# One input load of a dilated convolution split into sixteen DMAs, fourteen of them of two or three partitions

## The chip, the cores and the metric

The kernel runs on one NeuronCore of a Trainium2 chip. The metric is device time in microseconds, the median of several runs; less is better. Beside it stands a profile of one execution, whose span runs from the first to the last instruction.

## The reference

A 3x3 convolution with dilation 2 and padding 2, in float32: x is 16 x 64 x 64 x 64 (batch, channels in, rows, columns), weight 128 x 64 x 3 x 3, the output 16 x 128 x 64 x 64.

```python
for b in range(batch):
    for co in range(c_out):
        for ci in range(c_in):
            for kh in range(k):
                for kw in range(k):
                    output[b, co] += weight[co, ci, kh, kw] * x_pad[b, ci, kh*dilation:kh*dilation+h, kw*dilation:kw*dilation+w]
```

## The kernel before

Two images make a pair: their 2 x 64 input channels fill the 128 partitions, so there are `NP` = 8 pairs (0 to 7). A pair's input is a tile `x16` of 128 partitions x 64 rows x 64 columns in float16. Pair 0 comes as float32 in two DMAs from SyncE (L75) into a tile `x32` and is converted on VectorE and ScalarE; the others come by one DMA each from GpSimd's queue, which converts from float32 on the way (`load`, L78 to L81). A whole load reads 16 KB and writes 8 KB per partition.

The three kernel rows are computed with a trick that saves matmuls: GpSimd adds rows that lie two apart in the image (`prepare`, L141, tile `s16`), two instructions for a pair, for image rows 0 to 36 and 36 to 64. PE multiplies these sums with the middle kernel row (phase "w1"), and the rows themselves with differences of kernel rows (the other two phases). ScalarE copies the first phase from PSUM to SBUF (L204), and VectorE adds that copy to each of the two other phases and writes the output tile `o` (L209). A pair is walked in `NU` = 4 steps `u` of three phases each. All matmuls are issued on L186. The output tile of a pair is 4 MB and leaves by SyncE's queue: whole for pairs 0 to 4 (L221), by image for pairs 5 and 6, and by image and half for pair 7 (L224).

The buffers set how far engines may run ahead: `x16pool` has 6 tiles, `sumpool` (the sums) 3, `opool` (the outputs) 3. Pairs 1 to 4 are loaded near the start. Pairs 5, 6 and 7 are loaded two pairs ahead, at step u = 1 of pairs 3, 4 and 5 (L195), just in front of the two `prepare` calls of the next pair on GpSimd's queue. The order of the instructions on each engine is that of the program. Since GpSimd has to wait for PE only when a sum buffer is to be used again, it runs well ahead of PE: it fills the sums of pair p + 3 as soon as those of pair p have been read. Each DMA that GpSimd issues reports its landing on one of eight semaphores, taken in turn; a DMA that takes a semaphore again waits for the DMA that had it before.

Of the kernel before, what the change touches and what calls it, by code (L numbers as in the profile page):

```python
# [10 lines left out]
def kernel(  # L11
# [7 lines left out]
    nc = tc.nc  # L19

    B, CI, H, W = x.shape
# [5 lines left out]
    P = 128  # L27
    f32 = mybir.dt.float32
    f16 = mybir.dt.float16
    NP = B // 2  # L30
# [19 lines left out]
    x16pool = ctx.enter_context(tc.tile_pool(name="x16pool", bufs=6))  # L50
# [9 lines left out]
    x_pair = x.rearrange("(nb two) c h w -> nb (two c) h w", two=2)  # L60
# [5 lines left out]
    x16 = {}  # L66
# [11 lines left out]
    def load(pb, cuts):  # L78
        x16[pb] = x16pool.tile([P, H, W], f16, tag="x16", name=f"x16_{pb}")
        for lo, hi in zip(cuts, cuts[1:]):  # L80
            nc.gpsimd.dma_start(out=x16[pb][:, lo:hi], in_=x_pair[pb, :, lo:hi])  # L81

    AHEAD = 5

# [15 lines left out]
    for name, a in (("w21", 2), ("w01", 0)):  # L100
        for u in range(2):
            eng = nc.vector if name == "w21" else nc.gpsimd
            eng.tensor_sub(  # L103
                out=w16[:, SLOT[name] * KW : (SLOT[name] + 1) * KW, u, :],
                in0=w32k[:, a * KW : (a + 1) * KW, :],
                in1=w32k[:, KW : 2 * KW, :],
            )

            if name == "w01" and u == 0:
                load(1, [0, H])  # L110

    w_sb = wpool.tile([P, NS * KW, CO], f16, name="w_sb")
    for n, name in enumerate(("w1", "w21", "w0", "w01", "w2")):
        ps = cpool.tile([P, 2, NB], f32, tag="ps", name=f"wt{n}")
        k0 = SLOT[name] * KW
        for j in range(KW):
            nc.tensor.matmul(  # L117
                out=ps[:, 0, j * CO : (j + 1) * CO],
# [16 lines left out]
    def prepare(pb, lo, hi):  # L135
        if pb not in s16:
            s16[pb] = sumpool.tile([P, 2 * NQ, W], f16, tag="s16", name=f"s16_{pb}")
        src = (x16[pb] if pb else x32).rearrange("p (q e r) w -> p q e (r w)", e=2, r=2)
        dst = s16[pb].rearrange("p (q r) w -> p q (r w)", r=2)
        q0, q1 = lo // 4, hi // 4  # L140
        nc.gpsimd.tensor_add(  # L141
            out=dst[:, q0:q1], in0=src[:, q0:q1, 0, :], in1=src[:, q0:q1, 1, :]
        )

    prepare(0, 0, 20)
    for pb in range(2, AHEAD):
        load(pb, [0, H])
# [33 lines left out]
    def phase(pb, u, terms):  # L181

        ps = cpool.tile([CO, 2, NB], f32, tag="ps", name="ps")
        for pair in zip(*(conv(pb, hb, ps[:, hb], u, terms) for hb in range(2))):
            for m in pair:
                nc.tensor.matmul(**m)  # L186
        return ps

    BOTH = NP - 3
    for pb in range(NP):  # L190
        o = opool.tile([P, 2, H, W], f32, tag="o", name=f"o{pb}")
        ov = o.rearrange("p b (q e r) w -> p b q e (r w)", e=2, r=2)
        for u in range(NU):

            if u == 1 and AHEAD <= pb + 2 < NP:  # L195
                load(pb + 2, [0, H])
            if pb + 1 < NP:
                if u == 1:
                    prepare(pb + 1, 0, 36)
                elif u == 2:  # L200
                    prepare(pb + 1, 36, H)

            s32 = spool.tile([P, 2, NB], f32, tag="s32", name="s32")
            nc.scalar.copy(out=s32, in_=phase(pb, u, [("w1", 2, 0)]))  # L204
            for e, terms in enumerate(
                ([("w21", 1, 0), ("w0", 1, -1)], [("w01", 0, 0), ("w2", 0, 1)])
            ):
                ps = phase(pb, u, terms)
                nc.vector.tensor_add(  # L209
                    out=ov[:, :, u * UQ : (u + 1) * UQ, e, :],  # L210
                    in0=ps.rearrange("p b (q c) -> p b q c", c=QW),
                    in1=s32.rearrange("p b (q c) -> p b q c", c=QW),
                )

            step = NU // 2 if pb == NP - 1 else NU
            if (u + 1) % step == 0:
                fl = slice((u + 1 - step) * 4 * UQ, (u + 1) * 4 * UQ)
                if pb < BOTH:  # L220
                    nc.sync.dma_start(out=out_pair[pb], in_=o)  # L221
                else:
                    for hb in range(2):
                        nc.sync.dma_start(out=out[2 * pb + hb, :, fl], in_=o[:, hb, fl])  # L224
# [35 lines left out]
```

## Time and profile before

| | before |
|---|---|
| time, median of 3 runs | 126.64 us (126.33 to 126.74) |
| span of the profiled execution | 124.3 us |
| PE busy | 105.2 us (85%) |
| VectorE busy | 80.8 us (65%) |
| ScalarE busy | 39.6 us (32%) |
| GpSimd busy | 41.4 us (33%) |
| DMA moved | 43.42 MB in 3961 packets |
| HBM read, written | 17.07 MB, 33.55 MB |
| a load by GpSimd's queue, issue to landing | 16.0 us (median of 7) |

The span is that of one execution, from its first to its last instruction; the timed runs cover some time around it as well, and no time of the profiled execution apart from its span was recorded. "Busy" leaves out the issuing of DMAs. DMA bytes are counted as written: a load that converts float32 to float16 counts half of what it reads. "q0 software_dynamic" is the queue of the DMAs that GpSimd issues, "q1 hardware_dynamic" that of SyncE. Of the queues the profile gives packets, bytes and the time that the packets took as a share of the 16 DMA engines' time; in a window these are the packets that start in it. A line of the windows' table has for each engine the busy time in that stretch and the number of instructions, then the clock that PE was granted, the mean busy share of the 16 DMA engines, and the rate. A line of the timeline has start and duration, the engine, the line of the kernel, the operation, and in brackets the idle time before it and what ended it.

### The profile page before, as it was taken

The numbers are of one execution on the slowest core, as the hardware profiler recorded it, in microseconds if no ns is written. First come the engines' busy times: TensorE is split into PE (matmuls) and PEld (weight loads), VectorE is DVE, ScalarE is ACT, GpSimd is POOL, SyncE is SP. The second block draws the span as 40 slices with busy tenths as digits, with TensorE's granted clock in tenths as the row PEclk, the third lists the DMA queues.
The fourth block names the chain that finished last, engine by engine and source line by source line (L and its number), as shares of the span: only waits on it lengthen the run. The fifth ranks groups of instructions, "written<-read, shape, count | busy, mean of one in ns | idle before, by whom it ended". The sixth has DMA issues, their size and how long they took to land.

```text
span 124.3 us, 2244 instructions
## 1 busy us (share of the span) xinstructions
PE 105.2 (85%) x981; PEld 55.7 (45%) x981; DVE 80.8 (65%) x71; ACT 39.6 (32%) x40; POOL 41.4 (33%) x33
## 2 busy tenths in 40 slices
PE   6357999999999999999999999999999999960000
PEld 2043555555555555555555555555555555520000
DVE  0470199787778777877769778777877787770000
ACT  4760823333333333333333333333332433320000
POOL 2859998794095009500930093000000000000000
PEclk9999999999999999999999999999999999999655
DMA  4999999999999999999999999999999999999991
GB/s 129 346 359 218 214 214 216 224 237 411 393 327 314 332 306 319 316 390 314 324 345 427 425 427 432 422 427 427 432 438 427 432 414 432 427 417 419 422 406 71
DMA packets 3961, 43.42 MB, mean 349 GB/s; under 512 B 368, under 2 KB 368, under 8 KB 624
## 3 DMA queue, kind: packets, MB, share of 16 engines
q1 hardware_dynamic: 2944, 35.95, 68.9%
q0 software_dynamic: 1008, 7.34, 28.4%
q8 instruction: 7, 0.11, 0.3%
q14 instruction: 2, 0.02, 0.0%
HBM read 17.07 MB, written 33.55 MB: 407 GB/s over the span
## 4 chain that ended last, share of the span: by engine, by line
PE 80%; DMA 5%; POOL 2%; DVE 1%; DVEq 1%; SPq 0%; issue 0%
PE ps L186 80%; DMA x<-in_x_dram 5%; POOL s L141 2%; DVE o L209 1%; DVEq L255 1%; SPq L64 0%; DVEq L209 0%
## 5 line engine op out<-in xcount | busy, mean ns | idle before, releaser
L209 DVE TENSOR_TENSOR o<-ps,s 128x1024 f32<-128x1024 f32 x64 | 76.7, 1223 | 25.9 <-PE ps L186 16.8
L186 PE MATMUL ps<-x,w_sb 64*128 64x496 f16 (+3 forms) x768 | 85.3, 368 | 0.0
L186 PEld LDWEIGHTS <-w_sb 64*128 64x128 f16 x960 | 53.4, 95 | 49.3 <-issue 3.7
L204 ACT COPY s<-ps 128x1024 f32<-128x1024 f32 x32 | 32.4, 1012 | 63.0 <-PE ps L186 63.0
L141 POOL TENSOR_TENSOR s<-x 128x1152 f16<-128x1152 f16 (+4 forms) x18 | 35.1, 1971 | 31.1 <-PE ps L186 28.3
L186 PE MATMUL ps<-s,w_sb 64*128 64x496 f16 (+1 forms) x192 | 26.5, 379 | 2.1 <-POOL s L141 2.1
L81 POOL DMA_DIRECT2D x<-in_x_dram x7 | 4.0, 579 | 0.0
L132 ACT CAST x<-x 128x1024 f16<-128x1024 f32 (+1 forms) x3 | 2.8, 973 | 3.4 <-DMA x<-in_x_dram 3.4
L93 PE MATMUL warm<-zero 128*128 128x512 f16 x6 | 2.7, 630 | 1.2 <-DVE zero L87 1.2
L117 PE MATMUL wt<-ident,w 128*128 128x128 f16 x15 | 1.8, 312 | 2.1 <-ACT w L99 2.1
L103 DVE TENSOR_TENSOR w<-w 128x192 f16<-128x192 f32 x2 | 1.5, 800 | 2.5 <-DMA w<-in_weight_dram 2.5
L117 PEld LDWEIGHTS <-w 128*128 128x128 f16 x15 | 1.5, 146 | 3.0 <-ACT w L99 3.0
L99 ACT CAST w<-w 128x576 f16<-128x576 f32 x2 | 2.3, 1222 | 1.6 <-DMA w<-in_weight_dram 1.6
L103 POOL TENSOR_TENSOR w<-w 128x192 f16<-128x192 f32 x2 | 1.9, 951 | 2.4 <-DMA w<-in_weight_dram 2.4
L126 DVE CAST w_sb<-wt 128x384 f16<-128x384 f32 x3 | 1.6, 552 | 1.4 <-PE wt L117 1.4
L93 PEld LDWEIGHTS <-zero 128*128 128x128 f16 x6 | 0.7, 138 | 2.3 <-DVE zero L87 1.2
L99 ACT ACT_TABLE_LOAD x1 | 1.3, 1283 | 0.7 <-PEq L241 0.7
L128 ACT CAST w_sb<-wt 128x384 f16<-128x384 f32 x2 | 1.0, 478 | 1.1 <-PE wt L117 1.1
L130 DVE CAST x<-x 128x1280 f16<-128x1280 f32 x1 | 0.8, 826 | 0.5 <-DMA x<-in_x_dram 0.5
L87 DVE MEMSET zero<- 128x256 uint32 x1 | 0.3, 272 | 0.9 <-PEq L241 0.9
masks.py:199 POOL TENSOR_SCALAR_AFFINE_SELECT ident<-ident 128x128 f16<-128x128 f16 x1 | 0.3, 292 | 0.1
masks.py:197 POOL MEMSET ident<- 128x128 f16 x1 | 0.2, 204 | 0.3 <-POOLq L241 0.3
(4 smaller groups left out, 0.4 us busy)
## 6 DMA issues: line engine op xcount, KB each, us to landing
out_dram<-o SPq DMA_DIRECT2D x5, 4096.0 KB, 21.6
out_dram<-o SPq DMA_DIRECT2D x4, 2048.0 KB, 12.4
x<-in_x_dram POOLq DMA_DIRECT2D x7, 1024.0 KB, 16.0
out_dram<-o SPq DMA_DIRECT2D x4, 1024.0 KB, 10.6
x<-in_x_dram SPq DMA_DIRECT2D x1, 1152.0 KB, 6.5
x<-in_x_dram SPq DMA_DIRECT2D x1, 896.0 KB, 10.6
w<-in_weight_dram SPq DMA_DIRECT2D x1, 288.0 KB, 2.9
```

The source lines that it names most:

```text
L81: nc.gpsimd.dma_start(out=x16[pb][:, lo:hi], in_=x_pair[pb, :, lo:hi])
L93: nc.tensor.matmul(out=warm[:, 0], lhsT=zero[:, 0:P], rhs=zero, start=True, stop=True)
L99: nc.scalar.copy(out=w16[:, 0:NK, u, :], in_=w32k)
L103: eng.tensor_sub(out=w16[:, SLOT[name] * KW : (SLOT[name] + 1) * KW, u, :], in0=w32k[:, a * KW : (a + 1) * KW, :], in1=w32k[:, KW : 2 * KW ...
L117: nc.tensor.matmul(out=ps[:, 0, j * CO : (j + 1) * CO], lhsT=w16[:, k0 + j, :, :].rearrange("o t i -> o (t i)"), rhs=ident, start=True, st ...
L126: nc.vector.tensor_copy(out=dst, in_=ps[:, 0, 0 : KW * CO])
L132: nc.scalar.copy(out=x16[0][:, lo:hi], in_=x32[:, lo:hi])
L141: nc.gpsimd.tensor_add(out=dst[:, q0:q1], in0=src[:, q0:q1, 0, :], in1=src[:, q0:q1, 1, :])
L186: nc.tensor.matmul(**m)
L204: nc.scalar.copy(out=s32, in_=phase(pb, u, [("w1", 2, 0)]))
L209: nc.vector.tensor_add(out=ov[:, :, u * UQ : (u + 1) * UQ, e, :], in0=ps.rearrange("p b (q c) -> p b q c", c=QW), in1=s32.rearrange("p b ( ...
L255: with _tile.TileContext(nc) as tc:
```

## The change

The load of the last pair (7) goes through a new function. Instead of one DMA for the whole tile it issues sixteen: rows 0 to 60 of all 128 partitions; rows 60 to 64 of the first 112 partitions; and these four rows of the last 16 partitions twice half by half: the left 32 columns by eight DMAs of two partitions, the right 32 columns by five DMAs of three partitions and one of the single partition left. All pieces together cover the tile once. Nothing else is touched.

```diff
+    def load_tagged(pb):
+        x16[pb] = x16pool.tile([P, H, W], f16, tag="x16", name=f"x16_{pb}")
+        lo, p1 = H - 4, P - 16
+        parts = [(0, P, 0, lo, 0, W), (0, p1, lo, H, 0, W)]
+        for n, c in ((2, 0), (3, W // 2)):
+            parts += [
+                (p, min(n, P - p), lo, H, c, c + W // 2) for p in range(p1, P, n)
+            ]
+        for p, n, r, r1, c, c1 in parts:
+            nc.gpsimd.dma_start(
+                out=x16[pb][p : p + n, r:r1, c:c1],
+                in_=x_pair[pb, p : p + n, r:r1, c:c1],
+            )
...
             if u == 1 and AHEAD <= pb + 2 < NP:
-                load(pb + 2, [0, H])
+                if pb + 2 < NP - 1:
+                    load(pb + 2, [0, H])
+                else:
+                    load_tagged(pb + 2)
```

## The prediction

> **What bounds the kernel now.** I read the 40 slices first, then a table of windows, the DMA queues in three windows, the chain, and GpSimd's instructions in order of time.
>
> ```profile
> PE   6357999999999999999999999999999999960000
> DMA  4999999999999999999999999999999999999991
> GB/s 129 346 359 218 214 214 216 224 237 411 393 327 314 332 306 319 316 390 314 324 345 427 425 427 432 422 427 427 432 438 427 432 414 432 427 417 419 422 406 71
> ```
>
> PE stops in slice 36 of 40; the DMA engines are full from the second slice to the last but one. The GB/s dip in the first half only because loads are counted by what they write: they read float32 and write half as many bytes (8 loads read the 16.8 MB that are nearly all of "HBM read 17.07 MB"). Slices 4 to 8 at 214 to 218 written are about 430 read, the same as the outputs' 427.
>
> ```profile
> core 0: us, PE busy (x) PEld busy (x) DVE busy (x) ACT busy (x) POOL busy (x), PEclk, DMA share, GB/s
> 64.00:80.00 16.00, 16.00 (x157) 8.47 (x155) 13.19 (x12) 5.06 (x5) 4.21 (x2) 1.00 1.01 425
> 112.00:120.00 8.00, 0.00 (x0) 0.00 (x0) 0.01 (x1) 0.00 (x0) 0.00 (x0) 0.72 1.01 425
> 120.00:124.30 4.30, 0.00 (x0) 0.00 (x0) 0.00 (x0) 0.00 (x0) 0.00 (x0) 0.50 0.34 143
> ```
>
> After 112 us only DMA runs: 8.0 x 425 + 4.3 x 143 is 4.0 MB. The last two outputs (2.1 MB) are issued at 112.04, so 1.9 MB is queued ahead of them, 4.5 us at 427 GB/s. The chain says PE 80%, but it starts from the last engine instruction: PE, VectorE and all in front of them may slip 4.5 us before the DMA engines run dry. So the time is total work of the DMA engines over their rate, on the engine that ends last. The last window is uneven: mean busy there is 0.34 x 4.3 = 1.5 us, yet something runs to nearly 124, so an average engine ends some 2 us before the last.
>
> **Time.** The page gives only the span, 124.3 us; the timed runs have a median of 126.64, so 2.3 us lie around it. I add to both alike. One measurement of this kernel can tell about 0.3%, 0.38 us, from no change.
>
> **The change.** Pair 7's load, one DMA, becomes 16: 60 rows of 128 partitions, four rows of 112, then 8 DMAs of two partitions and 6 of at most three, each 4 rows x 32 columns. The bytes are the same. Three things are added.
>
> *GpSimd's time and waits.* Its part of the trace:
>
> ```profile
> 46.58 4.21 POOL L141 TENSOR_TENSOR s<-x 128x1152 f16<-128x1152 f16 x2 [7.65 <-PE ps L186]
> 50.73 0.57 POOL L81 DMA_DIRECT2D x<-in_x_dram  x1
> 58.95 4.21 POOL L141 TENSOR_TENSOR s<-x 128x1152 f16<-128x1152 f16 x2 [7.65 <-PE ps L186]
> 71.31 4.21 POOL L141 TENSOR_TENSOR s<-x 128x1152 f16<-128x1152 f16 x2 [8.14 <-PE ps L186]
> ```
>
> The load is issued at 50.73, right after pair 5's sums; GpSimd then sits idle until PE frees a sum buffer at 58.95. Fifteen more issues at 0.57 are 8.6 us (535 to 697 ns in the group's rows). But the order of the changed kernel shows more: GpSimd's DMAs share eight semaphores in turn, so the ninth to sixteenth DMA of this load each wait for an earlier DMA on their semaphore. The eighth waits for load 6 (issued 38.36, 17.5 us to landing, 55.9); the ninth for the 60-row DMA, which landed as a whole load after 16.0 us, at 66.7. Behind it on GpSimd are pair 6's sums and then pair 7's. Eight issues from 66.7 end at 71.3. If each of the six small DMAs queued by then lands one by one behind output packets, two turns of 0.61 us each, it is 66.7 + 7.3 + 0.6 = 74.6. Pair 6's sums then end at 75.5 to 78.8 instead of 63.2. PE runs from 9.95 for 99.61 us, 12.45 a pair, and wants them at 84.7; pair 7's sums (at most 4.2 us plus some 6 us until the last small DMA has landed, about 85 to 89) are wanted at 97.1. Cover: 6 us on the first, 8 on the second, and 4.5 us more of queued output behind both. Cost zero; without cover it would be a microsecond per microsecond.
>
> *Waits on PE.* Two weight loads and a matmul of pair 7 wait for eight semaphores where none stood; VectorE's queue shows 21 ns for such a wait, so 0.2 us, below the 4.5 us of queued output. Zero.
>
> *DMA work.* This has no cover: the engines are full. The packet counts:
>
> ```profile
> DMA packets 392, 2.83 MB, mean 217 GB/s; under 512 B 48, under 2 KB 48, under 8 KB 48
> q0 software_dynamic: 391, 2.81, 103.6%
> ...
> DMA packets 703, 10.73 MB, mean 429 GB/s; under 512 B 48, under 2 KB 48, under 8 KB 48
> q1 hardware_dynamic: 701, 10.70, 100.3%
> ...
> DMA packets 143, 0.37 MB, mean 284 GB/s; under 512 B 13, under 2 KB 13, under 8 KB 133
> q1 hardware_dynamic: 143, 0.37, 97.5%
> ```
>
> These are the queues in 12 to 25 us (loads alone), 75 to 100 (outputs alone) and 1.6 to 2.9 (the weights' rows of 2.3 KB). The page's 368 packets under 512 B are 16 for each of its 23 DMAs: one completion per engine.
>
> - Completions: 15 DMAs more, 15 on each engine if small ones also post 16. Price: the loads carry 48 of them to 343 data packets, the outputs 48 to 653, yet they read 432 GB/s (2 x 2.81 MB in 13 us) against 429. So the floor is zero; half a per cent of a 0.61 us packet over the difference of 0.07 a packet gives 0.045 us at most. I take 0.02, the middle: 0.30 us (0 to 0.7).
> - Small packets: 16 partitions x 4 rows x 2 halves, 128 of 128 B read, 8 on each engine if evenly spread. By bytes alone 128 B cost 0.005 us (0.613 us for 16 KB in the second window); the weights' packets cost 0.975 x 1.3 x 16 / 143 = 0.142. I take 0.04, nearer to the completions, whose size is nearer: 0.32 us (0.04 to 1.1).
> - The 112-partition piece: 7 packets more an engine at 0.01, its bytes being the same: 0.07 (0 to 0.3).
>
> The sum is 0.69 us, with ends of 0.04 and 2.1: 126.64 + 0.7 = 127.3, span 125.0.
>
> The Trainium skill (DMA: Bandwidth & Descriptors, section Anatomy of one DMA — SWDGE (gpsimd) path) gives a DMA of this kind a fixed cost of about 2.0 us; if that held the engines, 15 more DMAs would make 30 us and the kernel about 157. The trace speaks against it as a cost of engine time: in 12 to 25 us one load follows another at 432 GB/s read. It can only lengthen landings.
>
> **Rivals.**
>
> *Nothing measurable (0.17):* the completions are free and small packets cost little beyond bytes; 0.04 to 0.3 us, 126.8. For it: no window shows a price of a completion. Against: no row shows 128 B packets at the price of their bytes, and the weights' rows run at 284 GB/s.
>
> *Not slower (0.12): the last engine is relieved.* The end belongs to the engine that finishes last, and an average one has 2 us left. Should that engine have carried the last 16 partitions, and the small DMAs now go to others, it loses up to its whole share of the four rows: 8 partitions x 1 KB of read, half a packet, 0.31 us; 126.3. This decides from the point where its 15 completions cost under 0.02 each. The uneven last window speaks for it; nothing shows which engine is last.
>
> *Small pieces pile up on few engines (0.13).* If a two-partition DMA always goes to the first two engines and a three-partition one to the first three, the first engine gets 14 x 4 = 56 small packets: 56 x 0.04 + 0.37 = 2.6 us. On the last engine that is 129.2; on an average one, 2 us of it vanish in its slack: 127.2. Middle 128.2. No row of this profile has a DMA under 128 partitions, so it can't be excluded.
>
> The Trainium skill (same page, section Why a DMA increments its semaphore by 16 and not by 1) has both: few engines from a cursor that moves on, or, for some direct copies, one partition to an engine from the first on; by the first the pieces come out even, 127.3, by the second it is this rival. It also says that all 16 engines post a completion whatever the shape, as I assumed; no row here shows it for small ones.
>
> *GpSimd comes too late (0.05).* If each of the eight waits took far longer than two turns, pair 6's first sums would start after 82.2 and PE would stall; only beyond 4.5 us of stall, GpSimd free at 86.7, does it reach the end. At 89 it would be 2.3 us: 126.64 + 0.7 + 2.3 = 129.6. Against: 12 us to spare.
>
> That the pieces would not be there is no rival: the order of instructions has all 16.
>
> **How the numbers follow.** Even spread with priced packets has 0.53 and gives the time, 127.3, its own range 126.7 to 128.7. Slower: 0.51 of it, all of piling up (0.13) and of late GpSimd (0.05), 0.03 of the third case: 0.72. Same: 0.02 + 0.14 + 0.03 of relief = 0.19. Faster: 0.09 of relief, its 0.31 us being close to 0.38 and the runs lying 0.4 us apart. The range 126.5 to 128.8 leaves out most of relief, the upper half of piling up and late GpSimd: 0.2.
>
> **What would show it.** Packets up from 3961 to about 4441, those under 512 B from 368 to 736 (16 x 38 + 128); DMA slices still full, PE's end within a microsecond of 109.6, and the drain after it longer by the sum. GpSimd: eight issues from 50.7, a gap until about 66, eight more, pair 6's sums at 71 to 75. Wrong would be: a PE wait for the sums, a DMA slice below full, a drain of unchanged length (packets free), or completions that don't grow by 16 a DMA.

## The result, and the profile after

The changed kernel takes 131.25 us (median of 4 runs) against 126.48 before (four runs now as well): 4.77 us more by the medians. Medians here and below are over all runs, while a ratio leaves out a kernel's runs that lie over 1.5% above its fastest, here the one of 132.64: it is 1.0346 with a 95% interval of 1.031 to 1.0382, which is 4.4 us. The forecast was 127.3 and its range ended at 128.8. The profiled execution has a span of 129.7 us, 5.4 more than the 124.3 of before.

The slices of the page, the changed kernel:

```profile
PE   6289999999999999999999999930899999993000
...
PEclk9999999999999999999999999995589999999855
DMA  4999999999999999999999999999999607999993
GB/s 129 366 329 210 217 212 215 220 280 419 336 328 321 308 323 331 349 337 295 368 411 430 425 415 430 425 420 420 430 435 410 253 8 323 455 435 387 422 412 157
```

Three things are new, in this order of time: a hole in PE's row, a fall of the clock granted to PE right behind it, and a hole in the DMA row, with 8 GB/s in one slice. The same stretches as a table of windows (stretch, its length, busy time of PE, PE's weight loads, VectorE, ScalarE and GpSimd with their instructions, PE's clock, DMA share, GB/s):

```profile
84.00:88.00 4.00, 1.48 (x16) 0.76 (x13) 2.35 (x2) 0.20 (x1) 0.54 (x1) 1.00 1.03 430
88.00:92.00 4.00, 0.63 (x4) 0.30 (x5) 0.00 (x0) 0.00 (x0) 3.59 (x3) 0.50 0.99 418
92.00:96.00 4.00, 4.00 (x28) 1.90 (x26) 0.95 (x1) 1.01 (x1) 3.46 (x2) 0.65 1.02 426
96.00:104.00 8.00, 8.00 (x80) 4.11 (x76) 6.33 (x6) 2.43 (x3) 0.00 (x0) 1.00 0.84 343
104.00:108.00 4.00, 4.00 (x44) 2.16 (x40) 2.93 (x3) 1.62 (x2) 1.89 (x1) 1.00 0.15 63
```

PE does 2.1 us of work in the eight from 84 to 92, and the DMA engines go dry from 102 to 108, when the outputs of that time should have left. Why PE stands still, GpSimd's instructions in order of time say, here from the eighth of the sixteen issues on (the first seven start at 49.96):

```profile
55.23 0.54 POOL L92 DMA_DIRECT2D x<-in_x_dram  x1 [1.41 <-DMA x<-in_x_dram]
65.99 0.54 POOL L92 DMA_DIRECT2D x<-in_x_dram  x1 [10.22 <-DMA x<-in_x_dram]
71.24 0.54 POOL L92 DMA_DIRECT2D x<-in_x_dram  x1 [4.71 <-DMA x<-in_x_dram]
74.27 0.55 POOL L92 DMA_DIRECT2D x<-in_x_dram  x1 [2.49 <-DMA x<-in_x_dram]
76.74 0.55 POOL L92 DMA_DIRECT2D x<-in_x_dram  x1 [1.92 <-DMA x<-in_x_dram]
79.80 0.54 POOL L92 DMA_DIRECT2D x<-in_x_dram  x1 [2.52 <-DMA x<-in_x_dram]
82.87 0.54 POOL L92 DMA_DIRECT2D x<-in_x_dram  x1 [2.53 <-DMA x<-in_x_dram]
85.33 0.54 POOL L92 DMA_DIRECT2D x<-in_x_dram  x1 [1.93 <-DMA x<-in_x_dram]
88.39 0.54 POOL L92 DMA_DIRECT2D x<-in_x_dram  x1 [2.52 <-DMA x<-in_x_dram]
88.95 6.50 POOL L155 TENSOR_TENSOR s<-x 128x1152 f16<-128x1152 f16 x3
```

The last nine issues wait for landings, 30.2 us in all, and pair 6's sums start at 88.95 instead of 58.95. The list of waits and the chain complete it:

```profile
PE ps L200 <- POOL s L155: 5.9, 1, 5.9
...
88.95 2.38 POOL s L155
...
91.37 25.49 PE ps L200 x228
```

The packets that made the landings late are in the table of queues, first over the span, then from 75 to 88 us:

```profile
DMA packets 5162, 43.43 MB, mean 335 GB/s; under 512 B 1456, under 2 KB 1568, under 8 KB 1952
q0 software_dynamic: 2208, 7.34, 28.1%
...
q1 hardware_dynamic: 354, 5.54, 100.0%
q0 software_dynamic: 354, 0.00, 1.8%
```

GpSimd's queue has 1200 packets more than the 1008 of before, where the forecast had 480. From 75 to 88 us it and the outputs' queue start 354 packets each. This reads as turns: a packet of 4 to 64 bytes, then an output packet of 16 KB, and so on.

The theory formed on this, called A in the experiments: every small packet takes one turn behind an output packet of 0.61 us; a small DMA has five of them on every engine; GpSimd, whose DMAs wait for landings on their eight semaphores, is therefore late with pair 6's sums; PE stalls, and the outputs' queue runs dry. Rival B: the added packets' own work on the DMA engines makes the time, as in the forecast, at a higher price.

### The profile page after: what moved, and what is told of

It is laid out like the page before. It is cut to its first block, busy times and chain, and to the rows that moved or that the text cites. A ratio compares the mean times of both kernels' runs of the same rounds, so it can differ in the third digit from the quotient of the medians.

```text
span 129.7 us, 2266 instructions
## 1 busy us (share of the span) xinstructions
PE 107.7 (83%) x981; PEld 55.7 (43%) x981; DVE 81.9 (63%) x71; ACT 39.5 (30%) x40; POOL 49.4 (38%) x48
## 4 chain that ended last, share of the span: by engine, by line
PE 48%; DMA 29%; POOL 9%; issue 3%; DVE 1%; DVEq 1%; SPq 0%; POOLq 0%
PE ps L200 48%; DMA x<-in_x_dram 29%; POOL s L155 6%; POOL x L92 3%; DVE o L226 1%; DVEq L272 1%; SPq L64 0%; POOLq L155 0%; DVEq L226 0%
## 5 line engine op out<-in xcount | busy, mean ns | idle before, releaser
L200 PE MATMUL ps<-x,w_sb 64*128 64x496 f16 (+3 forms) x768 | 87.0, 373 | 0.2 <-DVE o L226 0.2
L155 POOL TENSOR_TENSOR s<-x 128x1152 f16<-128x1152 f16 (+4 forms) x18 | 34.5, 1936 | 23.7 <-DMA x<-in_x_dram 12.1
L200 PE MATMUL ps<-s,w_sb 64*128 64x496 f16 (+1 forms) x192 | 27.1, 386 | 6.4 <-POOL s L155 6.4
L92 POOL DMA_DIRECT2D x<-in_x_dram x16 | 8.7, 553 | 30.2 <-DMA x<-in_x_dram 30.2
L81 POOL DMA_DIRECT2D x<-in_x_dram x6 | 3.8, 642 | 0.0
L144 DVE CAST x<-x 128x1280 f16<-128x1280 f32 x1 | 1.9, 1922 | 0.0
## 6 DMA issues: line engine op xcount, KB each, us to landing
out_dram<-o SPq DMA_DIRECT2D x5, 4096.0 KB, 22.5
```

What stands on the lines that cost most here:

```text
L92: nc.gpsimd.dma_start(out=x16[pb][p : p + n, r:r1, c:c1], in_=x_pair[pb, p : p + n, r:r1, c:c1],)
L144: nc.vector.tensor_copy(out=x16[0][:, 0:20], in_=x32[:, 0:20])
L155: nc.gpsimd.tensor_add(out=dst[:, q0:q1], in0=src[:, q0:q1, 0, :], in1=src[:, q0:q1, 1, :])
```

## The experiments

**The same sixteen DMAs, fewer packets** (e1_rows). The four rows of the last 16 partitions are halved by rows instead of by columns, so that a piece is one run per partition.

```diff
-        for n, c in ((2, 0), (3, W // 2)):
+        for n, r in ((2, lo), (3, lo + 2)):
             parts += [
-                (p, min(n, P - p), lo, H, c, c + W // 2) for p in range(p1, P, n)
+                (p, min(n, P - p), r, r + 2, 0, W) for p in range(p1, P, n)
             ]
```

> The same sixteen DMAs with the same waits on GpSimd, but the last 16 partitions' four rows are cut in halves by rows instead of by columns, so that a piece is one run of 256 B written per partition instead of four of 64 B. Theory A (GpSimd is late because every packet of a small DMA takes its turn behind an output packet of 0.61 us; five packets an engine and DMA with the changed kernel, two here): the small DMAs land about 1.2 us apart instead of 2.5 to 3.1, GpSimd starts pair 6's sums at about 79 to 81 us instead of 89, PE wants them at 84 to 85, no stall, 126.7 to 127.2 us. Rival B (the work of the added packets on the DMA engines makes the time): the packets added fall from 1201 to about 580, half the loss stays, about 128.5 to 129. Rival C (the number of DMAs or of waits on GpSimd makes the time): 131, as with the change.

Measured: 127.15 us, ratio 1.0071 (1.0047 to 1.0096). GpSimd's queue, and its last waits in the timeline:

```profile
q0 software_dynamic: 1584, 7.34, 28.4%
...
77.22 0.51 POOL L92 DMA_DIRECT2D x<-in_x_dram  x1 [0.54 <-DMA x<-in_x_dram]
78.45 0.50 POOL L92 DMA_DIRECT2D x<-in_x_dram  x1 [0.72 <-DMA x<-in_x_dram]
79.66 0.51 POOL L92 DMA_DIRECT2D x<-in_x_dram  x1 [0.71 <-DMA x<-in_x_dram]
80.19 6.55 POOL L155 TENSOR_TENSOR s<-x 128x1152 f16<-128x1152 f16 x3
```

The issues that wait for small DMAs now follow 1.0 to 1.9 us apart, the last ones 1.2, which is two turns of 0.61; they were 2.5 to 3.1 apart. The sums start at 80.2, and no wait of PE for them is left. As many DMAs and as many waits on GpSimd cost 4.4 us (by the ratios) in one shape and 0.9 in the other: A holds. B, which left half the loss with about half the packets, and C, which left all of it, fall.

**The fourteen small DMAs with nobody waiting** (e2_offpath). Pair 7's load is one DMA again; the fourteen come after GpSimd's last sums, into a tile that nothing reads.

```diff
+    scr = wpool.tile([P, 4, W], f16, name="scr")
+
+    def small(pb):
...
                     prepare(pb + 1, 36, H)
+                    if pb + 2 == NP:
+                        small(NP - 1)
```

The body of `small`, left out here, issues the same fourteen pieces into `scr`.

> Pair 7 comes by one DMA as before; the same fourteen small DMAs are issued after pair 7's sums, the last work of GpSimd, into a scratch tile that nothing reads. The output is that of the kernel before. It measures the fourteen small DMAs' work with nobody waiting. Theory A: only the engines' time for some 1070 added packets, 14 x 5 an engine at 0.009 us for the four-byte ones and 0.026 us for the 64 B ones: about 0.7 to 0.9 us, so 127.2 to 127.5. Rival B (the packets make the time): 130 to 131. GpSimd's issues stretch from about 75 us to about 105, the last landing at 118 or so, before the outputs' end.

Measured: 127.72 us, ratio 1.0097 (1.0065 to 1.013), so 1.2 us. Its queue has 2080 packets, 1072 more than before and 67 on an engine: 0.018 us each, if they lie evenly on the 16 engines. The expected 0.7 to 0.9 was a little low. GpSimd's issues were again 2.5 to 3.9 us apart.

**Lateness without packets** (e3_delay20). Pair 7's load is one DMA, followed by twenty additions on GpSimd into a tile that nothing reads.

```diff
+                if pb + 2 == NP - 1:
+                    for _ in range(20):
+                        nc.gpsimd.tensor_add(
+                            out=scr, in0=x16[pb][:, 0:14], in1=x16[pb][:, 14:28]
+                        )
```

> Pair 7 comes by one DMA as before, with no packet added; between it and pair 6's sums GpSimd does twenty additions of 128x896 into a scratch tile that nothing reads, about 37.6 us, so that pair 6's sums start near 89 us as with the change. The output is that of the kernel before. Theory A (lateness of GpSimd alone makes PE stall and the outputs' queue run dry): PE stalls some 6 us before pair 6, the DMA engines go idle for 4 to 5 us near 100 us, 130 to 131 us. Rival B (packets): 126.5, as before.

Measured: 132.62 us, ratio 1.0491 (1.0455 to 1.0527): more than the change itself, with not one packet added. Its page and its chain:

```profile
DMA  5999999999999999999999999999999107999993
DMA packets 3961, 43.42 MB, mean 331 GB/s; under 512 B 368, under 2 KB 368, under 8 KB 624
...
91.65 26.69 PE ps L187 x228
```

The hole in the DMA row is like that of the changed kernel. The stall is 5.8 us against 5.9; PE's matmuls of pairs 6 and 7 (228 in the chain) take 26.69 us instead of 25.49, because the low clock lasted longer into them. These 1.2 us are most of the 1.3 by which the span, 131.0, exceeds that of the change. Lateness of GpSimd is enough for the whole loss.

**Two smaller delays** (e6_delay16 and e7_delay18: the same with sixteen and eighteen additions).

> As the kernel with twenty additions in front of pair 6's sums, with sixteen: GpSimd starts these sums near 82 us and has the first half at 84, just when PE wants it. The output is that of the kernel before. Theory A: no stall or one below 0.5 us, 126.3 us, no change. A rival by which the lateness of GpSimd costs before PE is late (its additions slow other engines or the DMA's): 127.5 to 131.

> With eighteen additions: the first half of pair 6's sums is ready near 88.3 us, PE stalls some 3 us. The outputs of pair 5 land at 103.2 us in the kernel before and those of pair 6 are issued at 99.75, so 3.5 us of output are queued there. Theory A: a stall of 3 us fits under it, 126.3 to 126.9 us; if PE's clock falls with so short a stall too, 1.7 us come on top and 127 to 128 remain. A rival without such a reserve (each microsecond of stall counts): 129 to 130.

With sixteen the sums start at 83.1 and nothing is lost that can be told: 126.68 us, ratio 1.0014 (0.9995 to 1.0033). GpSimd was 24 us later than before and busy all that time, at no cost. With eighteen the median is 128.62 us and the twelve runs lie from 126.71 to 130.82; the ratio is 1.0074 (1.0031 to 1.0117). The median is above the 127 to 128 that was expected if the clock falls too. The profiled execution (128.60) has a span of 126.8, a stall of 3.0 us, and the clock fell: 0.78, 0.50 and 0.87 in steps of 2 us from 88 to 94, which adds up to 3.4 us at half the clock. So a stall of 3 us can take the clock with it. Only one execution was profiled, but the mean granted clock of every run is on record: 0.969 to 0.975 in the three runs near 127 (126.71 to 126.96), and 0.956 to 0.959 in the four from 128.20 to 128.65. Half of 3.4 us is 0.013 of the span, so the difference fits one such fall. The five runs from 129.00 up (0.931 to 0.960) do not follow this and stay unexplained.

These kernels give one line for the end. The outputs of pair 6 were issued at the following times:

| | pair 6's outputs issued | span | difference |
|---|---|---|---|
| before | 99.75 | 124.3 | 24.5 |
| eighteen additions | 104.33 | 126.8 | 22.5 |
| the change | 107.02 | 129.7 | 22.7 |
| twenty additions | 108.51 | 131.0 | 22.5 |

Where the queue ran dry, the span ends 22.5 to 22.7 us after that issue. Before, it ends 24.5 after it: the reserve of queued output at that place is about 2 us, not the 3.5 that was read off the landing of pair 5's outputs when the run with eighteen additions was planned. The bytes agree: from 99.75 us on, the outputs' queue of the kernel before starts 9.22 MB, of which the outputs of pairs 6 and 7 are 8.39; the other 0.83 MB are 1.9 us at 427 GB/s.

**Small column pieces without waits** (e5_seven). The last 16 partitions come by five DMAs, seven in all.

```diff
-        for n, c in ((2, 0), (3, W // 2)):
+        for n, c in ((8, 0), (6, W // 2)):
```

> Pair 7 comes by seven DMAs instead of sixteen: the two large ones of the change, and the last 16 partitions' four rows by half the columns as in the change, but by two DMAs of eight partitions and three of six, six and four. The pieces stay 64 B and five packets an engine and DMA; with seven DMAs none has to wait for a semaphore of this load, so GpSimd does pair 6's sums at 59 us as before the change. Theory A (the waits in front of the sums make the loss, each packet added costs an engine about 0.02 us): some 33 packets more an engine, 0.6 to 0.7 us, 126.9 to 127.2 us. Rival B (small column pieces themselves make it): about half the change's loss, 128.5.

Measured: 126.73 us, ratio 1.0021 (1.0001 to 1.0041), 0.3 us. GpSimd did pair 6's sums at 57.8 us. The packets grew by 528, 33 an engine, nearly as many as the 36 of the variant by rows, which lost 0.9. So a packet cost 0.01 us here, 0.025 there; the difference between these two is not explained.

**Filling the stall on PE** (e4_warm on the change, e8_delay20_warm on the twenty additions).

```diff
+        if pb == NP - 2:
+            fill = cpool.tile([P, 2, NB], f32, tag="ps", name="fill")
+            for _ in range(16):
+                nc.tensor.matmul(
+                    out=fill[:, 0], lhsT=zero[:, 0:P], rhs=zero, start=True, stop=True
+                )
```

> The change as it is, with sixteen matmuls of zeros (128x512, a result that nothing reads) on PE just in front of pair 6, to fill the stall of about 6 us. The granted clock of PE in the changed kernel fell to 0.5 for 6.8 us around the stall, of which 3.4 us were pair 6's first matmuls. Theory A with the clock as a part of it: the clock stays at 1.0, PE gains 1.7 us on pair 6 and all behind it, 129.3 to 130 us. If the clock has no part (the DMA or the sums set the pace there): 131, as with the change, or later if the filling is longer than the stall.

> Twenty additions as in the kernel that measured 132.62 us, and the sixteen matmuls of zeros (a result that nothing reads) on PE in front of pair 6, 3.6 us of the stall of 5.8. The clock should stay at 1.0 as it did with this filling before. Theory A with the clock's part: pair 6 to 7 on PE shorter by 1.7 us, 130.5 to 131.3 us. If the clock has no part: 132.6. If the filling itself makes the kernel late, as the slower time with it suggests: 134 or more.

The clock stayed at 1.00 in both, and PE's matmuls of pairs 6 and 7 took 23.82 us in both; the chain of the second:

```profile
92.44 23.82 PE ps L187 x228
```

That is 1.7 us less than in the change and 2.9 less than with twenty additions: the low clock's price on PE is shown. But the kernels did not get faster. On the change it is 134.53 us (ratio 1.0649, 1.0598 to 1.07) against its ratio of 1.0346, so slower; on the twenty additions 134.31 (1.0515, 1.0446 to 1.0584; the runs lie from 132.38 to 135.42) against 1.0491, no change that can be told. In the first the whole run was late from the start (pair 5's sums at 48.55 us instead of 45.80), which outweighs the gain; why is not shown.

Both also lost time at the end. Pair 6's outputs were issued at 108.26 and 106.45 us, and the spans, 132.6 and 130.6, end 24.3 and 24.2 us later instead of 22.5 to 22.7, though the queue had run dry in both. The windows of the last DMA work show where the 1.6 us went, first with the filling, then with the twenty additions alone:

```profile
127.10:128.90 1.80, 0.00 (x0) 0.00 (x0) 0.00 (x0) 0.00 (x0) 0.00 (x0) 0.50 0.06 23
...
127.60:129.30 1.70, 0.00 (x0) 0.00 (x0) 0.00 (x0) 0.00 (x0) 0.00 (x0) 0.50 0.93 386
```

With the filling a share of 0.06, one engine of 16, works on alone for 1.8 us; without it all engines end together. The filling on the change has the same 0.06 from 129.00 to 130.75 us. So most of what PE had gained beside the twenty additions, outputs 2.1 us earlier, was lost again on one late DMA engine. Why it is late stays open: both kernels load eight packets of instructions on queue q8 where the others load seven, and the eighth (16 KB, 0.9 us) comes while the last outputs leave, but it is shorter than the delay.

## Why the prediction was wrong, point by point

**What bounds the kernel.** This was right for the kernel before: the DMA engines are full, and added packets show in the time when nothing else does (1.2 us for fourteen small DMAs off the path). It was wrong for the changed kernel, which is bound by GpSimd's waits from 50 to 89 us, then by PE, then by the outputs.

**The time of the landings: the step that failed.** The rival "GpSimd comes too late" came true; it had 0.05. The order of the sixteen issues and who waits behind them were right: the ninth issue, put at 66.7, came at 65.99. The failing term is "two turns of 0.61 us each" for a small DMA. It has five turns, on every engine if its packets lie evenly, so also on an engine that gets none of its data. The count of packets says so: 13 small DMAs of 80 packets and one, that of the single partition, of 32 are the 1072 measured off the path, and 80 is five for each of 16 engines, where I had counted one completion and the data alone. Five DMAs of 80 beside the 112-partition piece's 128 also give the 528 of the variant with seven. The profile does not name engines, but the landings fit: five turns are 3.05 us, and the issues were 2.5 to 3.1 apart. With runs of 256 B it was 32 per DMA, two an engine: the forecast's assumption on the landings, and the time then was 127.15, near the forecast's 127.3.

The piece of 112 partitions was left out of that chain altogether. It has seven data packets and a completion on each engine, eight turns, 4.9 us; measured from the ninth issue to the tenth: 5.25. So the same number of turns decided whether the runs were of 64, 256 or 512 B: two took about 1.2 us, five 2.5 to 3.1, eight 5.25. GpSimd's last issue was not at 74.0 but 4.9 + 6 x 2.75 after 66, at 87 to 88, with 2.75 as the middle of what was measured. Measured: 88.39. Two of the prediction's own signs of being wrong were there: a PE wait for the sums, 5.9 us, and DMA slices below full.

The Trainium skill (DMA: Bandwidth & Descriptors, section Queues, rings and completion order) has the engine alternate between queues by packet, a packet being some 9 to 17 descriptors. A small DMA would then pass in one turn. The trace agrees on the alternation, 354 packets to 354, but not on the size of a turn: each small packet that the profile counts in GpSimd's queue was one of its own.

**The cover.** 4.5 us of queued output was read in front of the last two outputs. Where the stall strikes, a pair earlier, it is about 2. And a stall has a price beyond its length: the clock. For these two reasons the price that the rival of the late GpSimd had for sums at 89 us, 129.6, was too low as well. The stall of 5.9 us and 1.7 of low clock are 7.6 us; pair 6's outputs came 7.3 later (107.02 after 99.75), less the reserve of 2 is 5.3, and the span grew by 5.4. On the low clock the Trainium skill (TensorE: Matmul & The Clock Gate, section Part 1) says that it comes after an idle window of about 3.4 us. The traces agree only in part: here the clock fell near 88.0, about 2.5 us after PE had stopped at 85.5, and with eighteen additions it fell at a stall of 3.0 us.

**DMA work.** The price of 0.02 us a packet was within what the runs show (0.01 to 0.025); the number, 30 an engine, should have been 75. In the changed kernel this work costs next to nothing all the same: it was done before the queue ran dry, and the idle time behind it would have been there in any case. With the twenty additions, which add none, the same line from issue to end holds.

**The other rivals.** The rival "nothing measurable" is refuted. That the last engine is relieved, or that pieces pile up on few engines, could not be seen: the profile does not name engines, and the 80 packets per DMA leave open which engines carried data.

## What to carry to other kernels

In these runs a DMA of a few bytes on a queue that shares its engines with large packets landed late in proportion to the packets it put on an engine, 0.6 us each, however little it moved. Count the packets, then look who waits: the engine that issues more DMAs than it has semaphores waits for landings, and everything queued behind those issues waits with it. A reserve of queued work is to be read at the place where the delay will strike, not at the end of the span.

## What the runs showed of the hardware that was not expected

- A two-partition DMA of four 64 B runs per partition made 80 packets, five for each of the 16 engines if they lie evenly, and so did one of three, six or eight partitions; one run per partition made 32.
- A packet of 4 to 64 B in GpSimd's queue took one turn beside output packets of 16 KB, 0.61 us, though its own work was worth 0.01 to 0.025.
- A PE stall of 3.0 us took the granted clock to 0.5 in one profiled execution; with one of 5.9 us the clock was low from 88 until past 94 us, and PE lost 1.7 us after its work had arrived.
- Behind a filled stall one DMA engine of 16 worked on alone for 1.8 us at the end (share 0.06), which took back most of the time that PE had gained; why is not shown.
- GpSimd could be kept busy for 31 us more, with additions in front of pair 6's sums, without a cost that can be told (ratio 1.0014, 0.9995 to 1.0033).
